# Hymba trunk layer on one core: another order of products, loads and final scaling in the down stage

## The chip, the core and the metric

The program runs on one NeuronCore of a Trainium2 chip. TensorE does the matrix products, VectorE and ScalarE the elementwise work, and SyncE (SP) issues the DMAs. The metric is the device time of one execution in microseconds (us), lower is better. Three runs of the kernel before took 2121.44 to 2122.35 us, with a median of 2121.78 us.

## The reference

One decoder layer on 512 tokens of width 2048, behind 16 meta tokens, in float32:

```python
h = concatenate([meta, x])
h = h + hybrid_mixer(rmsnorm(h, norm_mix), w_in, b_f, conv_w, out_gain, w_out)
h = h + (silu(f @ w_gate) * (f @ w_up)) @ w_down      # f = rmsnorm(h, norm_ffn), D_FF = 5632
out = rmsnorm(h, final_norm)[16:]                      # y * rsqrt(mean(y*y) + 1e-6) * final_norm
```

The change concerns the product with `w_down` (5632 x 2048) and the last rmsnorm.

## The kernel before

Weights come from DRAM in blocks of 1 MB through a ring of three buffers (`wpool`, pool 0). Each block is used in units of 128 x 1024 elements: ScalarE writes a rounded part `hi` (line 145), VectorE the rest `lo` (line 146), and every float32 product is made of three matmuls (lines 174 to 176). Both the gate and up stage and the down stage multiply 2 x 2 blocks by Strassen's method in Winograd's form, that is seven products of sums and differences of blocks instead of eight.

The gate and up stage ends with its result in seven linear combinations ("forms") per group of rows, which it writes to DRAM; the down stage reads form number `o` into a tile `x{o}` (`load_form`, line 744). Each of the five groups of 1024 rows of `w_down` is worked off in two halves `q` of the columns. A half has four weight blocks, "11", "12", "21" and "22", and seven products; each has two units of twelve matmuls with 512 columns. The first half of the first group runs in the order `FIRST_DOWN`: product 1 needs block "11" and tile `x0`, product 2 block "21" and `x5`, product 7 blocks "12" and "22" and `x1`, product 3 block "22" and `x6`. Which blocks a product's sum takes is in `NEEDS`, and `last` says after which product a block's buffer is free.

The blocks alternate, three by three, between pool 0 and a second ring of three buffers, `wpool3` (pool 2), which exists only once the gate and up stage has given back its memory (line 1025). `load_to` loads ahead as far as buffers are free. So of the first half three blocks are loaded while gate and up still runs, and the fourth, "22", later.

All DMAs stand in the one queue of SP, which works strictly in the order written into the program: an instruction that waits holds up those behind it. A scheduler places the instructions of all engines at build time; its order need not be that of the source, and the pieces of it that matter here are shown with the change.

The last 512 rows of `w_down` go through plain products (`down_last`), each piece of 128 rows by 512 columns followed by `finish`. There ScalarE squares and sums it (line 798). Once a 128-row group `t` has all its pieces, a few instructions on 128 x 1 elements make the factor `l_`. For the groups 0 to 2 VectorE then scales four pieces by `l_` and the norm weights in one instruction each (line 819). The last group multiplies by the norm weights piece by piece (line 807) and shares the scaling between VectorE and ScalarE (lines 821 and 823). SP issues all output DMAs (line 824).

Of the kernel before, what the change touches and what calls it, by code (L numbers as in the profile page):

```python
# [12 lines left out]
ALU = mybir.AluOpType  # L13
AX = mybir.AxisListType

P = 128
# [14 lines left out]
RAW_BUFS = 3  # L31
# [4 lines left out]
def hymba_kernel(  # L36
# [17 lines left out]
    nc = tc.nc  # L54
    x = x[0]
    w_in, w_out, w_gate, w_up, w_down = (w[0] for w in (w_in, w_out, w_gate, w_up, w_down))
    out = out[0]

    const = ctx.enter_context(tc.tile_pool(name="const", bufs=1))
    wpool = ctx.enter_context(tc.tile_pool(name="wpool", bufs=RAW_BUFS))  # L60
# [31 lines left out]
    def later(*stages):  # L92
        pending.extend((state["done"], s) for s in stages)

    pools = [wpool, None, None]
    held = [[], [], []]
    bufs = (RAW_BUFS, 1, RAW_BUFS)

    def add_block_of(view, k, f, pool=0):
        blocks.append({"src": view, "k": k, "f": f, "pool": pool})  # L100
        return len(blocks) - 1
# [545 lines left out]
    def ring():  # L647
        return 2 * ((len(blocks) - n_gate_up_blocks) // 3 % 2)
# [1 line left out]

    TARGETS = {1: (1, 0, 1), 2: (1, 0, 1), 6: (0, 0, 1), 4: (0, 0, 1), 7: (0, 1, -1), 5: (0, 1, -1), 3: (1, 1, -1)}

    FIRST_DOWN = ((1, 1, "a"), (2, 6, "b"), (7, 2, "c"), (6, 3, "a"), (4, 4, "c"), (5, 5, "a"), (3, 7, "d"))
    NEEDS = {1: ("11",), 2: ("21",), 7: ("12", "22"), 6: ("12", "22"), 4: ("12", "22", "21"), 5: ("12",), 3: ("22",)}

    def down(c):
        for q in range(2):
            bs = {}
            for b in ("11", "22", "12", "21") if c or q else ("11", "21", "12", "22"):
                h, f0 = int(b[0]) - 1, q * 1024 + (int(b[1]) - 1) * 512  # L660
                view = w_down[c * 1024 : (c + 1) * 1024, f0 : f0 + 512].rearrange("(p two k) f -> two k p f", two=2, k=P)[h]
                bs[b] = add_block_of(view, NPAIR, 512, ring())
            down_products(c, q, bs)

    def down_products(c, q, bs):
        cell, touched = {}, set()
        order = GATE_UP if c or q else FIRST_DOWN

        def source(i, half):
            def part(b):  # L670
                return blocks[bs[b]]["view"][:, 2 * half : 2 * half + 2, :]

            def add(o, a, b):
                nc.vector.tensor_tensor(o, a, b, op=ALU.add)
                return o

            if i == 7:
                cell["sum", half] = shared["dsums"].tile([P, 2, 512], F32, tag=f"sum{half}", name=f"sum{half}")
                return add(cell["sum", half], part("12"), part("22"))
            if i == 6:  # L680
                return add(cell["sum", half], cell["sum", half], part("11"))
            if i == 4:
                return add(cell["sum", half], cell["sum", half], part("21"))
            if i == 5:
                return add(part("12"), part("12"), part("11"))
            return part({1: "11", 2: "21", 3: "22"}[i])

        def product(n, i, o, b, half, hi, lo):
            if half == 0 and c == q == 0:
                load_soon(n)  # L690
            start = b not in cell
            if start:
                cell[b] = [bank("mm" if b in "ad" else "aux") for _ in range(2)]
            x = form_tiles[c, o]
            for k in range(2):
                kp = 2 * half + k
                for j in range(2):
                    ts = slice(j * P, (j + 1) * P)
                    mm3(cell[b][j], (x[:, 0, kp, ts], x[:, 1, kp, ts]), (hi[:, k, :], lo[:, k, :]), start and k == 0, i in (2, 3, 4) and kp == NPAIR - 1, skip_group_check=True)
            if half == 0:  # L700
                return
            for a, f, sign in [TARGETS[i]] + [TARGETS[3]] * (i == 5 and order is FIRST_DOWN):
                if (a, 2 * q + f) not in accs:
                    accs[a, 2 * q + f] = shared["down"].tile([P, 2, 512], F32, tag=f"acc{a}{2 * q + f}", name=f"acc{a}{2 * q + f}")
                for j in range(2):
                    m = acc(2 * a + j, 2 * q + f)
                    if c == 0 and (a, f) not in touched:
                        nc.scalar.activation(m, cell[b][j], AF.Copy, scale=float(sign))
                    else:
                        nc.vector.tensor_tensor(m, m, cell[b][j], op=ALU.add if sign > 0 else ALU.subtract)  # L710
                touched.add((a, f))
            if q == 1:
                load_form(c + 1, o)
                if c == NDOWN - 1 and n in (1, 3, 5):
                    add_h(*((0, 0), (1, 0), (0, 1))[n // 2])

        last = {"11": 5, "12": 5, "21": 2, "22": 3} if c or q else {"11": 5, "12": 5, "21": 4, "22": 3}
        for n, (i, slot, b) in enumerate(order):
            for half in range(2):
                add_unit(bs["11"], slice(0, 2), slice(0, 512), lambda hi, lo, a=(n, i, slot - 1, b, half): product(*a, hi, lo), sum=lambda i=i, half=half: source(i, half), also=[bs[m] for m in NEEDS[i]], look=4)  # L720
        for b, i in last.items():
            blocks[bs[b]]["last"] = len(units) - 14 + 2 * [g[0] for g in order].index(i) + 1

    def after_block(n):

        return tc.issue_after(blocks[min(n, state["loaded"] - 1)]["dma"].ins)

    def load_soon(n):

        if n == 0:  # L730
            with after_block(n_gate_up_blocks + 3):
                load_form(0, 2)
                load_form(0, 3)
        elif n == 2:
            with after_block(n_gate_up_blocks + 4):
                load_form(0, 4)
                load_form(0, 6)

    form_tiles = {}

# [4 lines left out]
    def load_form(c, o):  # L745
        if c < NDOWN:
            x = x_tile(o).rearrange("p (n k t) -> p n k t", n=2, k=NPAIR)
            nc.sync.dma_start(x.bitcast(F32), shared["forms"][c][o])
            form_tiles[c, o] = x
        elif o < 2:  # L750
            last_hid[o] = x_tile(o).rearrange("p (k t) -> p k t", k=4)
            nc.sync.dma_start(last_hid[o].bitcast(F32), shared["last"][o])
# [39 lines left out]
    def finish(t, fb, cols, n, last):  # L792

        tail, fss = shared["tail"], shared["fss"][:, t, :]
        a = acc(t, fb)[:, cols]
        fnorm = shared["fnorm"]
        r = shared["rstd2c"][:, t : t + 1]
        nc.scalar.activation(shared["sq"][:, cols], a, AF.Square, scale=r, accum_out=fss[:, n : n + 1])
        end = t == NT - 1
        if last:  # L800
            u, v, h, l_, lr = (tail.tile([P, 1], F32, tag=tag, name=tag) for tag in ("fu", "fv", "fh", "fl", "fr"))
            nc.vector.reduce_sum(u, fss[:, :n], axis=AX.X)
            nc.vector.tensor_scalar(u, u, 1.0 / D, EPS, op0=ALU.mult, op1=ALU.add)
            nc.scalar.activation(l_, fss[:, n : n + 1], AF.Ln, bias=u, scale=1.0 / D)
            nc.vector.scalar_tensor_tensor(v, fss[:, n : n + 1], 1.0 / D, u, op0=ALU.mult, op1=ALU.add)
        if end:
            nc.vector.tensor_tensor(a, a, fnorm[:, fb * 512 + cols.start : fb * 512 + cols.stop], op=ALU.mult)
        if not last:
            return
        nc.scalar.activation(l_, l_, AF.Exp, scale=-0.5)  # L810
        nc.scalar.activation(lr, l_, AF.Copy, scale=r)
        nc.vector.tensor_scalar(h, v, -0.5, None, op0=ALU.mult)
        nc.vector.scalar_tensor_tensor(h, h, l_, l_, op0=ALU.mult, op1=ALU.mult)
        nc.vector.scalar_tensor_tensor(l_, h, 1.5, lr, op0=ALU.add, op1=ALU.mult)
        parts = ((0, 0, 256), (0, 256, 512), (1, 0, 512), (2, 0, 512), (3, 0, 512)) if end else [(f, 0, 512) for f in range(4)]
        for n, (f, a, b) in enumerate(parts):
            o = acc(t, f)[:, a:b]
            if not end:
                nc.vector.scalar_tensor_tensor(o, o, l_, fnorm[:, f * 512 : (f + 1) * 512], op0=ALU.mult, op1=ALU.mult)
            elif n % 2:  # L820
                nc.scalar.activation(o, o, AF.Copy, scale=l_)
            else:
                nc.vector.tensor_scalar(o, o, l_, None, op0=ALU.mult)
            nc.sync.dma_start(out[t * P : (t + 1) * P, f * 512 + a : f * 512 + b], o)

    for pair in range(D_FF // 256):
        gate_up(pair)
# [192 lines left out]
    shared["down"] = ctx.enter_context(tc.tile_pool(name="down", bufs=1, reuse_waits="tile"))  # L1020
    load_form(0, 0)
    load_form(0, 5)
    with after_block(n_gate_up_blocks + 2):
        load_form(0, 1)
    pools[2] = ctx.enter_context(tc.tile_pool(name="wpool3", bufs=RAW_BUFS, side="right", reuse_waits="tile"))
    shared["dsums"] = ctx.enter_context(tc.tile_pool(name="dsums", bufs=1, side="right", reuse_waits="tile"))
    shared["tail"] = ctx.enter_context(tc.tile_pool(name="tail", bufs=2, side="right", reuse_waits="tile"))
# [36 lines left out]
```

## Time and profile before

| | |
|---|---|
| median of the runs | 2121.78 us |
| the profiled execution's own time | 2121.52 us |
| its span | 2119.7 us |
| TensorE busy | 2093.8 us (99%) |
| VectorE busy | 1588.9 us (75%) |
| ScalarE busy | 925.2 us (44%) |
| DMA, mean over the span | 146 GB/s |

Times within the trace are counted from the start of the span. The chain that ended last belongs to TensorE for 93% of the span, so time is gained or lost where TensorE waits, and after its last matmul. Most of the program is a stretch in which it never waits; the two places that the change touches are the start of the down stage, at 1679 us, and the end, from 2064 us on.

### The profile page before, as it was taken

How to read it: one execution, taken by the hardware profiler on the slowest of the kernel's cores; microseconds unless marked ns; L12 is line 12 of the kernel's file. 1: busy time of each engine (PE TensorE's matmuls, PEld its weight loads, DVE VectorE, ACT ScalarE, POOL GpSimd, SP SyncE). 2: the span in 40 equal slices, each digit the busy share in tenths (PEclk: the TensorE clock that was granted, in tenths of full speed). 3: DMA queues.
4: the chain of work that ended last, by engine and by line, in shares of the span. 5: the costliest groups of instructions: out<-in, count | busy, mean ns of one | idle time of the engine just before them, and what ended most of it. 6: DMA issues, size and time to landing. Idle time of an engine off the chain costs nothing.

```text
span 2119.7 us, 34563 instructions
## 1 busy us (share of the span) xinstructions
PE 2093.8 (99%) x14556; PEld 1937.0 (91%) x14556; DVE 1588.9 (75%) x2071; ACT 925.2 (44%) x1252; POOL 25.9 (1%) x78
## 2 busy tenths in 40 slices
PE   8999999999999999999999999999999999999997
PEld 7999999999998887999999999999999988888886
DVE  4756656454446667888898888888988798988996
ACT  5233334222215554544554455445544454333343
POOL 0000100000000000000000000000000000000000
PEclk9999999999999999999999999999999999999999
DMA  6322222232323433445444454454444665665562
GB/s 196 103 65 91 85 85 80 80 100 80 100 92 127 158 120 107 143 150 179 151 157 151 155 175 143 149 181 147 159 153 155 231 258 186 238 217 170 212 225 90
DMA packets 230751, 309.77 MB, mean 146 GB/s; under 512 B 7396, under 2 KB 183852, under 8 KB 225716
## 3 DMA queue, kind: packets, MB, share of 16 engines
q1 hardware_dynamic: 230596, 307.57, 43.7%
q8 instruction: 114, 1.87, 0.4%
q14 instruction: 41, 0.34, 0.1%
HBM read 260.35 MB, written 47.20 MB: 145 GB/s over the span
## 4 chain that ended last, share of the span: by engine, by line
PE 93%; DMA 2%; DVE 2%; ACT 1%; SPq 1%; issue 0%; DVEq 0%; ACTq 0%
PE mm L174 22%; PE mm L175 22%; PE mm L176 22%; PE mm L273 17%; PE aux L176 3%; PE aux L175 3%; PE aux L174 3%; DMA y<-in_x_dram 1%; DMA x<-forms_dram 1%; DVE lo L146 1%; DMA hin<-h_dram 1%; PE aux L374 1%; DVE acc L710 0%; PE aux L472 0%; ACT hf L481 0%
## 5 line engine op out<-in xcount | busy, mean ns | idle before, releaser
L145 ACT CAST hi<-raw 128x1024 fp32r<-128x1024 f32 x388 | 407.7, 1051 | 611.6 <-PE mm L175 266.7
L146 DVE TENSOR_TENSOR lo<-raw,hi 128x1024 fp32r<-128x1024 f32 x388 | 473.2, 1222 | 235.8 <-ACT hi L145 234.2
L176 PE MATMUL mm<-hhi,lo 128*128 128x256 f32 x1848 | 514.0, 278 | 0.6 <-DVE lo L146 0.6
L174 PE MATMUL mm<-hhi,hi 128*128 128x256 f32 x1848 | 505.8, 277 | 0.5 <-ACT gate L580 0.5
L175 PE MATMUL mm<-hlo,hi 128*128 128x256 f32 x1848 | 503.7, 276 | 0.0
L176 PEld LDWEIGHTS mm<-hhi,lo 128*128 128x128 f32 x1848 | 346.7, 188 | 2.5 <-DVE lo L146 0.8
L174 PEld LDWEIGHTS mm<-hhi,hi 128*128 128x128 f32 x1848 | 345.6, 188 | 2.0 <-ACT gate L580 2.0
L175 PEld LDWEIGHTS mm<-hlo,hi 128*128 128x128 f32 x1848 | 345.6, 188 | 0.0
L145 ACT CAST hi<-sum 128x1024 fp32r<-128x1024 f32 x192 | 201.6, 1051 | 307.0 <-DVE sum L533 159.7
L146 DVE TENSOR_TENSOR lo<-sum,hi 128x1024 fp32r<-128x1024 f32 x192 | 234.7, 1222 | 59.4 <-ACT hi L145 57.8
L273 PE MATMUL mm<-xhi,hi 128*128 128x256 f32 (+2 forms) x1024 | 215.4, 284 | 0.0
L273 PE MATMUL mm<-xhi,lo 128*128 128x256 f32 (+2 forms) x1024 | 214.0, 284 | 0.7 <-DVE lo L146 0.7
L273 PE MATMUL mm<-xlo,hi 128*128 128x256 f32 (+2 forms) x1024 | 214.0, 284 | 0.0
L174 PE MATMUL mm<-ghi,hi 128*128 128x256 f32 x616 | 172.7, 281 | 3.4 <-ACT ghi L145 3.3
L175 PE MATMUL mm<-glo,hi 128*128 128x256 f32 x616 | 171.8, 279 | 0.4 <-DVE glo L146 0.4
L176 PE MATMUL mm<-ghi,lo 128*128 128x256 f32 x616 | 170.8, 277 | 0.0
L273 PEld LDWEIGHTS mm<-xhi,hi 128*128 128x128 f32 x1024 | 163.3, 189 | 0.8
L273 PEld LDWEIGHTS mm<-xlo,hi 128*128 128x128 f32 x1024 | 162.1, 189 | 1.5 <-issue 0.9
L273 PEld LDWEIGHTS mm<-xhi,lo 128*128 128x128 f32 x1024 | 161.8, 189 | 1.4 <-DVE lo L146 0.9
L175 PE MATMUL mm<-lo,x 128*128 128x512 f32 x352 | 137.3, 390 | 0.6 <-DVE lo L146 0.6
L176 PE MATMUL mm<-hi,x 128*128 128x512 f32 x352 | 137.1, 389 | 0.0
L174 PE MATMUL mm<-hi,x 128*128 128x512 f32 x352 | 123.8, 389 | 1.1 <-DMA x<-forms_dram 1.1
(245 smaller groups left out, 3487.7 us busy)
## 6 DMA issues: line engine op xcount, KB each, us to landing
raw<-in_w_in_dram SPq DMA_DIRECT2D x47, 1024.0 KB, 5.3
raw<-in_w_gate_dram SPq DMA_DIRECT2D x44, 1024.0 KB, 4.8
raw<-in_w_up_dram SPq DMA_DIRECT2D x44, 1024.0 KB, 5.1
raw<-in_w_down_dram SPq DMA_DIRECT2D x44, 1024.0 KB, 6.4
x<-forms_dram SPq DMA_DIRECT2D x35, 1024.0 KB, 7.3
forms_dram<-fhi SPq DMA_DIRECT2D x20, 896.0 KB
forms_dram<-flo SPq DMA_DIRECT2D x20, 896.0 KB, 4.8
raw<-in_w_out_dram SPq DMA_DIRECT2D x16, 1024.0 KB, 5.0
```

Source lines behind the costliest of these rows:

```text
L145: nc.scalar.copy(hi, src)
L146: nc.vector.tensor_tensor(lo, src, f32(hi), op=ALU.subtract)
L174: nc.tensor.matmul(o, lhi, rhi, start=start, stop=False, **kw)
L175: nc.tensor.matmul(o, lhi, rlo, start=False, stop=False, **kw)
L176: nc.tensor.matmul(o, llo, rhi, start=False, stop=stop, **kw)
L273: nc.tensor.matmul(ps[:, : b - a], lhs[:, k, :], rhs[:, kt, a:b], start=s0, stop=s1)
L374: nc.tensor.transpose(ps[:, (i - i0) * P : (i - i0 + 1) * P], pr[i][:, j * P : (j + 1) * P], ident)
```

## The change

The first half of the first group now runs its products in the order 1, 2, 3, 7, 6, 4, 5. Its blocks are loaded in the order "11", "21", "22", "12", so that the three loaded ahead are those of the products 1, 2 and 3, and the fourth, "12", has a buffer of its own in the pool `down` (pool 3). The tiles loaded when that pool opens are `x0`, `x5` and `x6`, then block "12", and after these `x1` to `x4`. In `finish` every piece, not only those of the last group, is multiplied by the norm weights as it comes; the final scaling is shared by VectorE and ScalarE for all groups; and for the last group the two DMAs of ScalarE's pieces are issued by ScalarE.

```diff
--- before.py
+++ after.py
@@ -92,9 +92,9 @@
     def later(*stages):
         pending.extend((state["done"], s) for s in stages)
 
-    pools = [wpool, None, None]
-    held = [[], [], []]
-    bufs = (RAW_BUFS, 1, RAW_BUFS)
+    pools = [wpool, None, None, None]
+    held = [[], [], [], []]
+    bufs = (RAW_BUFS, 1, RAW_BUFS, 1)
 
     def add_block_of(view, k, f, pool=0):
         blocks.append({"src": view, "k": k, "f": f, "pool": pool})
@@ -650,16 +650,17 @@
 
     TARGETS = {1: (1, 0, 1), 2: (1, 0, 1), 6: (0, 0, 1), 4: (0, 0, 1), 7: (0, 1, -1), 5: (0, 1, -1), 3: (1, 1, -1)}
 
-    FIRST_DOWN = ((1, 1, "a"), (2, 6, "b"), (7, 2, "c"), (6, 3, "a"), (4, 4, "c"), (5, 5, "a"), (3, 7, "d"))
+
+    FIRST_DOWN = ((1, 1, "a"), (2, 6, "b"), (3, 7, "d"), (7, 2, "c"), (6, 3, "a"), (4, 4, "c"), (5, 5, "a"))
     NEEDS = {1: ("11",), 2: ("21",), 7: ("12", "22"), 6: ("12", "22"), 4: ("12", "22", "21"), 5: ("12",), 3: ("22",)}
 
     def down(c):
         for q in range(2):
             bs = {}
-            for b in ("11", "22", "12", "21") if c or q else ("11", "21", "12", "22"):
+            for b in ("11", "22", "12", "21") if c or q else ("11", "21", "22", "12"):
                 h, f0 = int(b[0]) - 1, q * 1024 + (int(b[1]) - 1) * 512
                 view = w_down[c * 1024 : (c + 1) * 1024, f0 : f0 + 512].rearrange("(p two k) f -> two k p f", two=2, k=P)[h]
-                bs[b] = add_block_of(view, NPAIR, 512, ring())
+                bs[b] = add_block_of(view, NPAIR, 512, ring() if c or q or b != "12" else 3)
             down_products(c, q, bs)
 
     def down_products(c, q, bs):
@@ -714,7 +715,7 @@
                 if c == NDOWN - 1 and n in (1, 3, 5):
                     add_h(*((0, 0), (1, 0), (0, 1))[n // 2])
 
-        last = {"11": 5, "12": 5, "21": 2, "22": 3} if c or q else {"11": 5, "12": 5, "21": 4, "22": 3}
+        last = {"11": 5, "12": 5, "21": 2, "22": 3} if c or q else {"11": 5, "12": 5, "21": 4, "22": 7}
         for n, (i, slot, b) in enumerate(order):
             for half in range(2):
                 add_unit(bs["11"], slice(0, 2), slice(0, 512), lambda hi, lo, a=(n, i, slot - 1, b, half): product(*a, hi, lo), sum=lambda i=i, half=half: source(i, half), also=[bs[m] for m in NEEDS[i]], look=4)
@@ -729,12 +730,12 @@
 
         if n == 0:
             with after_block(n_gate_up_blocks + 3):
+                load_form(0, 1)
                 load_form(0, 2)
-                load_form(0, 3)
         elif n == 2:
             with after_block(n_gate_up_blocks + 4):
+                load_form(0, 3)
                 load_form(0, 4)
-                load_form(0, 6)
 
     form_tiles = {}
 
@@ -803,8 +804,7 @@
             nc.vector.tensor_scalar(u, u, 1.0 / D, EPS, op0=ALU.mult, op1=ALU.add)
             nc.scalar.activation(l_, fss[:, n : n + 1], AF.Ln, bias=u, scale=1.0 / D)
             nc.vector.scalar_tensor_tensor(v, fss[:, n : n + 1], 1.0 / D, u, op0=ALU.mult, op1=ALU.add)
-        if end:
-            nc.vector.tensor_tensor(a, a, fnorm[:, fb * 512 + cols.start : fb * 512 + cols.stop], op=ALU.mult)
+        nc.vector.tensor_tensor(a, a, fnorm[:, fb * 512 + cols.start : fb * 512 + cols.stop], op=ALU.mult)
         if not last:
             return
         nc.scalar.activation(l_, l_, AF.Exp, scale=-0.5)
@@ -815,13 +815,12 @@
         parts = ((0, 0, 256), (0, 256, 512), (1, 0, 512), (2, 0, 512), (3, 0, 512)) if end else [(f, 0, 512) for f in range(4)]
         for n, (f, a, b) in enumerate(parts):
             o = acc(t, f)[:, a:b]
-            if not end:
-                nc.vector.scalar_tensor_tensor(o, o, l_, fnorm[:, f * 512 : (f + 1) * 512], op0=ALU.mult, op1=ALU.mult)
-            elif n % 2:
+            if n % 2:
                 nc.scalar.activation(o, o, AF.Copy, scale=l_)
             else:
                 nc.vector.tensor_scalar(o, o, l_, None, op0=ALU.mult)
-            nc.sync.dma_start(out[t * P : (t + 1) * P, f * 512 + a : f * 512 + b], o)
+            queue = nc.scalar if end and n % 2 else nc.sync
+            queue.dma_start(out[t * P : (t + 1) * P, f * 512 + a : f * 512 + b], o)
 
     for pair in range(D_FF // 256):
         gate_up(pair)
@@ -1020,8 +1019,11 @@
     shared["down"] = ctx.enter_context(tc.tile_pool(name="down", bufs=1, reuse_waits="tile"))
     load_form(0, 0)
     load_form(0, 5)
-    with after_block(n_gate_up_blocks + 2):
-        load_form(0, 1)
+    load_form(0, 6)
+
+    pools[3] = shared["down"]
+    assert state["loaded"] == n_gate_up_blocks + 3
+    load_part(1)
     pools[2] = ctx.enter_context(tc.tile_pool(name="wpool3", bufs=RAW_BUFS, side="right", reuse_waits="tile"))
     shared["dsums"] = ctx.enter_context(tc.tile_pool(name="dsums", bufs=1, side="right", reuse_waits="tile"))
     shared["tail"] = ctx.enter_context(tc.tile_pool(name="tail", bufs=2, side="right", reuse_waits="tile"))
```

In the built program the places that follow read thus. First the queue of SP where the down stage begins, before the change. `raw` is a weight block (`raw_17822` the third of the stage, `raw_17917` the fourth, "22"), `x0` to `x6` are the forms' tiles, `last_dram` takes the last rows of the gate and up result (`fhi` and `flo`).

```order
L123 DMA raw_17822<-in_w_down_dram 128x4x512
L748 DMA x0_17900<-forms0_dram_6690 128x2048
L748 DMA x5_17902<-forms0_dram_6690 128x2048
L748 DMA x1_17904<-forms0_dram_6690 128x2048
L123 DMA raw_17917<-in_w_down_dram 128x4x512
L123 DMA raw_17919<-in_w_down_dram 128x4x512
L623 DMA last_dram_6689<-fhi_17885 128x1024
L123 DMA raw_17921<-in_w_down_dram 128x4x512
L748 DMA x2_17927<-forms0_dram_6690 128x2048
L623 DMA last_dram_6689<-flo_17886 128x1024
L748 DMA x3_17929<-forms0_dram_6690 128x2048
L748 DMA x4_18009<-forms0_dram_6690 128x2048
```

And the same place after the change, where `raw_17906` is the block "12" in its own place, and `raw_17919`, `raw_17921` and `raw_18199` are blocks of `wpool3` for the second half and the group behind it.

```order
L123 DMA raw_17822<-in_w_down_dram 128x4x512
L123 DMA raw_17919<-in_w_down_dram 128x4x512
L123 DMA raw_17921<-in_w_down_dram 128x4x512
L123 DMA raw_18199<-in_w_down_dram 128x4x512
L623 DMA last_dram_6689<-fhi_17885 128x1024
L623 DMA last_dram_6689<-flo_17886 128x1024
L749 DMA x0_17900<-forms0_dram_6690 128x2048
L749 DMA x5_17902<-forms0_dram_6690 128x2048
L749 DMA x6_17904<-forms0_dram_6690 128x2048
L123 DMA raw_17906<-in_w_down_dram 128x4x512
L749 DMA x1_17927<-forms0_dram_6690 128x2048
L749 DMA x2_17929<-forms0_dram_6690 128x2048
```

`x0` and `x5` stood directly behind the third block, ahead of the first block of `wpool3`; now they stand behind three blocks of `wpool3` and both writes to `last_dram`, and block "12" and the other forms behind them.

Next VectorE at the end of the program, before: `acc_18474`, `acc_18239`, `acc_17961` and `acc_18158` hold the four column blocks of the last two row groups; `fu` to `fr` are 128 x 1.

```order
L814 SCALAR_TENSOR_TENSOR fl<-fh,fr 128x1
L807 TENSOR_TENSOR acc_18474<-acc_18474,fnorm 128x256
L802 TENSOR_REDUCE fu<-fss 128x1
L819 SCALAR_TENSOR_TENSOR acc_17961<-acc_17961,fl,fnorm 128x512
L819 SCALAR_TENSOR_TENSOR acc_18158<-acc_18158,fl,fnorm 128x512
L819 SCALAR_TENSOR_TENSOR acc_18239<-acc_18239,fl,fnorm 128x512
L819 SCALAR_TENSOR_TENSOR acc_18474<-acc_18474,fl,fnorm 128x512
L763 TENSOR_TENSOR acc_18474<-acc_18474,mm 128x256
L803 TENSOR_SCALAR fu<-fu 128x1
L805 SCALAR_TENSOR_TENSOR fv<-fss,fu 128x1
L807 TENSOR_TENSOR acc_18474<-acc_18474,fnorm 128x256
```

And after; `acc_18042` is what was `acc_18158`.

```order
L814 SCALAR_TENSOR_TENSOR fl<-fh,fr 128x1
L821 TENSOR_SCALAR acc_17961<-acc_17961,fl 128x512
L821 TENSOR_SCALAR acc_18239<-acc_18239,fl 128x512
L764 TENSOR_TENSOR acc_18474<-acc_18474,mm 128x256
L807 TENSOR_TENSOR acc_18239<-acc_18239,fnorm 128x512
L764 TENSOR_TENSOR acc_18474<-acc_18474,mm 128x256
L807 TENSOR_TENSOR acc_18474<-acc_18474,fnorm 128x256
L803 TENSOR_REDUCE fu<-fss 128x1
L807 TENSOR_TENSOR acc_18474<-acc_18474,fnorm 128x256
L804 TENSOR_SCALAR fu<-fu 128x1
L806 SCALAR_TENSOR_TENSOR fv<-fss,fu 128x1
L812 TENSOR_SCALAR fh<-fv 128x1
```

Four scalings by line 819 stood between the additions of the two last pieces; now two of line 821 stand ahead of both, and the multiplication of the last piece (the second `L807` of `acc_18474` with 256 columns) comes before the scalar `L804`.

Last, ScalarE at the end of the program after the change, with its two DMAs.

```order
L799 ACTIVATE sq,fss<-acc_18239,rfa 128x512
L819 ACTIVATE acc_18042<-acc_18042,fl 128x512
L819 ACTIVATE acc_18474<-acc_18474,fl 128x512
L799 ACTIVATE sq,fss<-acc_18474,rfa 128x256 x2
L805 ACTIVATE fl<-fss,fu 128x1
L810 ACTIVATE fl<-fl 128x1
L811 ACTIVATE fr<-fl,rfa 128x1
L819 ACTIVATE acc_17961<-acc_17961,fl 128x256
L819 ACTIVATE acc_18239<-acc_18239,fl 128x512
L823 DMA out_dram<-acc_17961 128x256
L823 DMA out_dram<-acc_18239 128x512
```

The two scalings of group 2 (`L819`) are ScalarE's now, and stand ahead of the squares of the two last pieces.

## Rows read from the trace of the kernel before

**Rows 1.** Busy time by engine in three stretches, first row the columns.

```profile
core 0: us, PE busy (x) PEld busy (x) DVE busy (x) ACT busy (x) POOL busy (x), PEclk, DMA share, GB/s
1679.00:1700.00 21.00, 18.28 (x78) 13.88 (x77) 16.09 (x17) 8.67 (x11) 0.00 (x0) 1.00 0.99 347
1700.00:2064.00 364.00, 364.00 (x1607) 301.34 (x1606) 326.45 (x344) 151.03 (x151) 0.00 (x0) 1.00 0.60 214
2064.00:2109.00 45.00, 43.83 (x204) 36.35 (x202) 30.21 (x60) 17.01 (x43) 0.00 (x0) 1.00 0.17 59
```

**Rows 2.** Timeline, TensorE, where the down stage starts: start, length, instruction, idle before.

```profile
...
1679.02 0.39 PE L174 MATMUL mm<-hi,x 128*128 128x512 f32 x1
...
1690.48 0.73 PE L174 MATMUL aux<-hi,x 128*128 128x512 f32 x2 [0.41 <-ACT hi L145]
...
1692.47 0.50 PE L175 MATMUL aux<-lo,x 128*128 128x512 f32 x1 [1.26 <-DVE lo L146]
...
1699.00 0.70 PE L174 MATMUL mm<-hi,x 128*128 128x512 f32 x2 [1.05 <-DMA x<-forms_dram]
...
```

**Rows 3.** Timeline, queue of SP, same place.

```profile
...
1668.71 3.15 SPq L748 DMA_DIRECT2D x<-forms_dram  x3
1679.21 0.93 SPq L123 DMA_DIRECT2D raw<-in_w_down_dram  x2
1680.75 0.34 SPq L623 DMA_DIRECT2D last_dram<-fhi  x1
1681.13 2.09 SPq L123 DMA_DIRECT2D raw<-in_w_down_dram  x1
1683.26 0.75 SPq L748 DMA_DIRECT2D x<-forms_dram  x1
...
```

**Rows 4.** Chain that ended last, 1678 to 1706: start, length, what.

```profile
...
1683.26 15.60 DMA x<-forms_dram
...
```

**Rows 5.** Line 123 (weight blocks), 1640 to 1760: from issue to landing.

```profile
...
DMA to landing us min/median/max: 5.9/6.2/14.3
```

**Rows 6.** Line 748 (forms), 1640 to 1760: from issue to landing.

```profile
...
DMA to landing us min/median/max: 4.8/6.4/8.1
```

**Rows 7.** Timeline, VectorE, where the down stage starts.

```profile
...
1681.38 0.68 DVE L146 TENSOR_TENSOR flo<-up,fhi 128x512 fp32r<-128x512 f32 x1
...
1687.79 2.36 DVE L674 TENSOR_TENSOR sum<-raw 128x1024 f32<-128x1024 f32 x2 [3.47 <-DMA raw<-in_w_down_dram]
...
```

**Rows 8.** Stretches before the gate and up stage, where TensorE had waited.

```profile
...
830.00:834.00 4.00, 1.29 (x4) 0.99 (x5) 3.00 (x5) 2.18 (x3) 0.00 (x0) 0.59 0.00 0
834.00:838.00 4.00, 3.59 (x9) 1.65 (x8) 3.97 (x8) 1.34 (x3) 0.00 (x0) 0.56 0.00 0
...
```

**Rows 9.** Timeline, TensorE, its last matmul.

```profile
...
2108.18 0.28 PE L176 MATMUL mm<-x,x 128*128 128x256 f32 x1
```

**Rows 10.** Timeline, VectorE, last rows.

```profile
...
2108.62 2.73 DVE L819 SCALAR_TENSOR_TENSOR acc<-acc,fl,fnorm 128x512 f32<-128x512 f32 x4
2111.27 0.41 DVE L763 TENSOR_TENSOR acc<-acc,mm 128x256 f32<-128x256 f32 x1
...
2112.43 0.42 DVE L807 TENSOR_TENSOR acc<-acc,fnorm 128x256 f32<-128x256 f32 x1
...
2113.54 1.15 DVE L823 TENSOR_SCALAR acc<-acc,fl 128x256 f32<-128x256 f32 x3
```

**Rows 11.** Timeline, ScalarE, last rows.

```profile
...
2106.35 0.72 ACT L798 ACTIVATE sq<-acc,rfa 128x512 f32<-128x512 f32 x1 [0.17 <-DVE acc L763]
...
2111.72 0.51 ACT L798 ACTIVATE sq<-acc,rfa 128x256 f32<-128x256 f32 x1 [3.54 <-DVE acc L763]
...
2112.35 0.30 ACT L804 ACTIVATE fl<-fss,fu 128x1 f32<-128x1 f32 x1
...
2113.54 1.12 ACT L821 ACTIVATE acc<-acc,fl 128x256 f32<-128x256 f32 x2 [0.33 <-DVE fl L814]
```

**Rows 12.** Timeline, queue of SP, last issues.

```profile
...
2113.92 2.54 SPq L824 DMA_DIRECT2D out_dram<-acc  x5
```

## The prediction

> **What bounds the kernel now.** I read the busy times by stretch first, then TensorE's gaps on the timeline, then the queue of SP beside them, and last the three engines at the end. In [rows 1] the reader is to see that from 1700 to 2064 us TensorE is busy for 364.00 of 364.00 us: what the change does to VectorE, ScalarE or DMA there costs nothing unless it makes TensorE wait. 1607 matmuls in 364 us are 0.2265 us each, so a product of 24 takes 5.44 us. In the 21 us from 1679 TensorE is busy for 18.28 only. [Rows 2] show the gaps: 0.41 and 1.26 us before the third product, 1.05 before the fourth, 2.72 us together. The first product, at 1679.02, has no gap before it. [Rows 7] tell why the third is late: VectorE's sum of "12" and "22" waits until 1687.79 for the fourth block, which SP issued at 1679.21 only [rows 3]. The gap before the fourth product is the DMA of a form issued at 1683.26, 15.60 us before it ended [rows 4]. The end lies behind the last matmul (2108.46 [rows 9]): VectorE first does four scalings of 2.73 us and adds the last piece at 2111.27 [rows 10].
>
> **The change where the down stage begins.** Products 1, 2 and 3 need only the three blocks that are loaded early, so the wait for the fourth block goes, and with it the wait for the next form: −2.72 us if nothing else comes late. But every product needs its form too, and there the order rows of SP decide. Before, `x0`, `x5` and `x1` were issued from 1668.71 on [rows 3], ten microseconds before TensorE read `x0`, and nothing held them. Then SP stood still until 1679.21, when the first block of `wpool3` went out. That is 0.03 us after the last matmul of gate and up, which started 0.11 us before the 1679.02 of [rows 2] and ran 0.28 us: the block takes memory that this matmul still read. After the change `x0` stands behind that block. Nothing on SP can pass it, so `x0` cannot be issued before 1679.2, when TensorE already wants it. Ahead of `x0` stand three blocks (3 MB), then the two writes to `last_dram` (0.5 MB each), the second of which waits for `flo`, ready at 1681.38 + 0.68 = 1682.1 [rows 7].
>
> When does `x0` land? The first block, with the queue empty before it, needs the median 6.2 us [rows 5]: 1679.21 + 6.2 = 1685.4. The pace behind it I take from before. There the block issued at 1679.21 had landed by 1687.79 [rows 7], and behind it came a block, half a megabyte of `fhi`, a block and the form issued at 1683.26, which landed at 1683.26 + 15.60 = 1698.86 [rows 3, 4]. That is 3.5 MB in 11.1 us, 3.16 us per MB. After the change 4 MB stand behind the first block up to and with `x0` (two blocks, two writes, the form): 12.7 us, so `x0` lands at 1685.4 + 12.7 = 1698.1. The first product then starts 19.1 us later than at 1679.02. Bounds: if transfers did not queue behind each other, `x0` would be issued at about 1682.1 and land after the shortest time of a form, 4.8 us [rows 6], at 1686.9, 7.9 us late. If each of the three blocks took 6.2 us and the 2 MB behind them 6.3 us, it would be 1704.1, 25.1 us late. I take 19.1, since the transfers before ran in the same queue with nearly the same content.
>
> The Trainium skill, DMA: Bandwidth & Descriptors (Queues, rings and completion order), says that each DMA engine takes its descriptors in ring order, but that completion is not first in, first out for an issuing engine. By the first half the sum stands; by the second a form could overtake blocks. The 15.60 us of [rows 4] against 4.8 us for a form on its own speak for the first.
>
> Behind `x0` all later forms move too. `x5` and `x6` follow at 3.16 us each and their products at 5.44 us each, so they are in time. Block "12" is three megabytes behind `x0`, 9.5 us. VectorE takes its two sums (2.36 us [rows 7]) before the `lo` of product 3's first half (as long as one of the sums, 1.2 us): 13.1 us after `x0`, when two products need 10.9 us and the clock's 1.8 us (below) come on top, 12.7 us. I cost this wait at nothing; its upper bound, with "12" two microseconds later, is 2 us. `x1` to `x4` have the same margin or more.
>
> While TensorE waits, its clock falls. In [rows 8] it had waited and then worked for 3.59 of 4 us at a granted share of 0.56, that is most of the time at 1.2 GHz instead of 2.4. A restart of the same kind loses 4 × (1 − 0.56) = 1.8 us. Bounds: nothing, and 3.4 us if both rows (0.59 and 0.56 over 8 us) fell behind the restart.
>
> **The change at the end.** For the groups 0 to 2 twelve multiplications (0.42 us for 256 columns [rows 10], so up to 0.84 each) replace twelve scalings of 2.73 / 4 = 0.68 us, six short scalings come on VectorE and six on ScalarE. Until 2109 VectorE is busy for 30.21 and ScalarE for 17.01 of 45 us [rows 1], beside TensorE's matmuls, so this is hidden. What counts begins with the square at 2106.35 [rows 11]. ScalarE's order is now: that square, two scalings of group 2, the squares of the two last pieces. A square of 256 columns holds it 2112.35 − 2111.72 = 0.63 us, one of 512 columns 0.21 more. Two scalings take 1.12 + 0.21 = 1.33 us. So 2106.35 + 0.84 + 1.33 + 2 × 0.63 = 2109.8; the last addition, free now to follow the matmul at 2108.46 and 0.41 us long, is in time. Before, that was 2112.35. But now the last multiplication (0.42) and a small instruction (at most the 0.30 of line 804) stand between the square and the logarithm: 2110.5. From there to the scaling are 2113.54 − 2112.35 = 1.19 us, so 2111.7 instead of 2113.54, 1.8 us earlier. Behind it SP issued five outputs one by one in 2.54 us, until 2116.46 [rows 12]. Now SP issues three, done by about 2111.7 + 1.15 + 0.4 = 2113.3, and ScalarE two behind its 1.12 us. How long an issue takes on ScalarE this trace does not show. With SP's mean of 0.51 us each the end is 2113.8, a gain of 2.6 us; with SP's longest, 2.09 us [rows 3], it is 2117.0, a loss of 0.5. The megabyte itself must still pass, which may leave only the 1.8. I take −2.5, nearest to SP's own issues at this place, with −3.2 (SP's three alone) and +0.5 as bounds.
>
> The Trainium skill, DMA: Bandwidth & Descriptors (Issuing engines are not separate DMA queues), says that issuing from several engines saves only the time to issue. By that rule the second queue adds at most two issues of 0.51 us to the 1.8, 2.8 us in all.
>
> **Sum.** From the profiled execution's 2121.5 us: +19.1 (first form) +1.8 (clock) −2.7 (old gaps) −2.5 (end) = +15.7, so 2137.2. The median of the runs lies 0.26 above that execution: 2137.5 us. With all bounds on one side it would be 2121.8 + 7.9 − 2.7 − 3.2 = 2123.8, or 2121.8 + 25.1 + 3.4 + 2 + 0.5 = 2152.8 with the gaps back in another place.
>
> **The rivals.**
> - *The form overtakes.* The blocks ahead of `x0` are only beside it, and it lands within 4.8 to 8.1 us of an issue at 1682.1 to 1684: 1686.9 to 1692. The cost is then 7.9 to 13 us, with the clock and the gains +4.5 to +9.6: 2126 to 2131. For it speaks that forms issued one after another landed in 8.1 us at most where they could go early [rows 6]. Against it speaks the 15.60 us of [rows 4].
> - *The form is no bound (faster than before).* If `x0` were in its tile when gate and up ends, as before, both gains would stay: 2121.8 − 2.7 − 2.5 = 2116.6 us. The mechanism is the one that the change describes, three products from blocks at hand. It decides up to the point where the first wait is as long as both gains, 1679.0 + 5.2 = 1684.2. Against it: the shortest landing, 4.8 us, behind an issue that comes after `flo` is ready at 1682.1.
> - *The wait moves on.* The queue is slower than 3.16 us per MB since all seven forms and one more block are now in it at once. `x0` comes at 1704, and block "12" holds the third product for another 2 us: 2144 to 2150 us. For it: the 347 GB/s of [rows 1] are now wanted for 12 MB from 1679 on where there were 8. Against it: the queue is served in order, and what is added stands behind `x0`.
>
> **How the numbers follow.** The first, 2137.5 us with an own range of 2131 to 2144, has 0.77; the overtaking form 0.11; no bound at the form 0.05; the wait that moves on 0.07. The range of 8 in 10 is 2128 to 2144.5: it takes in the upper half of the overtaking case and the edge of the last. A measurement of this kernel can tell 0.2% (4.2 us) from no change. Faster by more than that (under 2117.5) is most of the third case, 0.04. Within it, up to 2126.0, is the rest of that case and the edge of the overtaking one, 0.04. Slower is 0.92.
>
> **What would show it.** In the profile after, TensorE has one gap of 14 to 25 us before the first matmul with 512 columns of the down stage, put down to a form's DMA. SP issues three blocks from 1679.2 on and the first form behind them. The granted clock falls in that stretch. Products 3 and 7 have no gap of a microsecond or more. From the last matmul to the end of the span it is about 2.5 us less than the 11.2 (2119.7 − 2108.46) of before. It would be wrong if the first form were issued before the last matmul of gate and up, or if TensorE's gap were under 8 us.

## The result and the profile after

The changed kernel takes 2137.69 us (median of four runs, 2135.67 to 2138.88); four runs of the kernel before on the same chip had a median of 2122.07 us. The ratio is 1.0068, with a 95% interval of 1.0056 to 1.0081: slower by 15.6 us. The profiled execution took 2138.88 us, with a span of 2137.1 us where before had 2119.7.

First TensorE's idle times in the changed kernel: for each kind of wait the sum, the count and the longest, in us, over the down stage.

```profile
engine line waited for: us in total, times, longest us
PE mm L174 <- DMA x<-forms_dram: 18.8, 1, 18.8
PE mm L175 <- DVE lo L146: 0.7, 1, 0.7
```

The three gaps of [rows 2] are gone; products 3 and 7 have none. One gap has come in their place. TensorE's timeline there (start, length, instruction, idle before and what ended it):

```profile
1681.33 0.28 PE L176 MATMUL mm<-ghi,lo 128*128 128x256 f32 x1
1700.39 0.79 PE L174 MATMUL mm<-hi,x 128*128 128x512 f32 x1 [18.78 <-DMA x<-forms_dram]
1700.98 0.63 PE L175 MATMUL mm<-lo,x 128*128 128x512 f32 x1
...
1704.39 0.63 PE L174 MATMUL mm<-hi,x 128*128 128x512 f32 x1
1704.82 0.50 PE L175 MATMUL mm<-lo,x 128*128 128x512 f32 x1
...
1707.00 0.39 PE L175 MATMUL mm<-lo,x 128*128 128x512 f32 x1
```

The last matmul of gate and up ends at 1681.6, and 18.8 us later the first product starts: it has waited for the DMA of a form. Behind the gap the matmuls first take 0.63 us each instead of 0.39. The queue of SP in the same stretch (start of the first issue, time over all of them):

```profile
1670.71 12.39 SPq L123 DMA_DIRECT2D raw<-in_w_down_dram  x4
1683.20 1.07 SPq L623 DMA_DIRECT2D last_dram<-fhi  x1
1684.50 0.48 SPq L623 DMA_DIRECT2D last_dram<-flo  x1
1685.04 2.08 SPq L749 DMA_DIRECT2D x<-forms_dram  x3
1687.51 0.38 SPq L123 DMA_DIRECT2D raw<-in_w_down_dram  x1
1691.49 8.28 SPq L749 DMA_DIRECT2D x<-forms_dram  x4
```

In [rows 3] three forms went out at 1668.71. Here one weight block goes out at 1670.71, the group of four lasts until 1683.10, then come both writes, and the first form at 1685.04, 3.4 us after TensorE has run out of matmuls. It is in use 15.4 us later. Of the group of four the last three, the blocks of `wpool3`, are issued from 1681.63 on, 0.02 us after the last matmul of gate and up has ended. What holds `x0` last is the second write, as the chain that ended last shows (start, length, what):

```profile
1683.87 0.61 DVE flo L146
1684.50 0.48 SPq L623
1685.04 15.31 DMA x<-forms_dram
```

The write of `flo` goes out as soon as `flo` is ready, 2.9 us after the last matmul of gate and up, and `x0` right behind it. The busy times by stretch (columns as in [rows 1]) show the clock and the bus meanwhile:

```profile
1679.00:1700.00 21.00, 2.60 (x23) 2.40 (x22) 5.16 (x8) 3.03 (x4) 0.00 (x0) 0.63 0.81 286
1700.00:1704.00 4.00, 3.61 (x9) 2.84 (x10) 0.00 (x0) 0.00 (x0) 0.00 (x0) 0.50 1.01 418
1704.00:1720.00 16.00, 16.00 (x70) 13.21 (x69) 12.79 (x13) 7.29 (x9) 0.00 (x0) 0.97 0.93 373
1720.00:2080.00 360.00, 360.00 (x1589) 297.74 (x1588) 322.70 (x339) 150.45 (x150) 0.00 (x0) 1.00 0.57 204
```

TensorE is busy for 2.60 of 21 us, where [rows 1] had 18.28. It restarts at a granted clock of 0.50, which is the level of 1.2 GHz. From 1720 on nothing waits again, as before from 1700.

Last the end: TensorE, VectorE, ScalarE with its two DMAs, and SP, from the last matmul on.

```profile
2128.27 0.28 PE L176 MATMUL mm<-x,x 128*128 128x256 f32 x1
```

```profile
2128.59 0.42 DVE L764 TENSOR_TENSOR acc<-acc,mm 128x256 f32<-128x256 f32 x1 [0.26 <-PE mm L176]
...
2129.67 0.43 DVE L807 TENSOR_TENSOR acc<-acc,fnorm 128x256 f32<-128x256 f32 x1 [0.17 <-ACT sq L799]
2130.01 0.15 DVE L804 TENSOR_SCALAR fu<-fu 128x1 f32<-128x1 f32 x1
...
2131.34 1.15 DVE L821 TENSOR_SCALAR acc<-acc,fl 128x256 f32<-128x256 f32 x3
```

```profile
2130.26 0.29 ACT L805 ACTIVATE fl<-fss,fu 128x1 f32<-128x1 f32 x1 [0.62 <-DVE fu L804]
...
2131.34 1.12 ACT L819 ACTIVATE acc<-acc,fl 128x256 f32<-128x256 f32 x2 [0.23 <-DVE fl L814]
2131.88 0.95 ACTq L823 DMA_DIRECT2D out_dram<-acc  x2
```

```profile
2121.58 11.44 SPq L823 DMA_DIRECT2D out_dram<-acc  x11
```

The scaling starts at 2131.34, 2.8 us behind the last matmul's end (2128.55); in [rows 9, 10] it was 5.1 us. SP's last issue ends at 2133.02 and ScalarE's at 2132.83, so the span ends 4.1 us behind SP's last issue. From the last matmul to the end of the span it is 8.5 us where it was 11.2.

So the spans differ by: +2.4 us before the down stage (gate and up ends at 1681.6 instead of 1679.2, spoken of at the very end), +18.9 us from the end of gate and up to the first product's start (18.78, and 0.16 that the two overlapped before), −1.3 us over the down stage (428.16 us from the first product's start to the last matmul's end, where it was 429.44), −2.7 us behind it. The sum is 17.4, which is 2137.1 − 2119.7.

### The profile page after: what moved, and what is told of

Same layout as the page of the kernel before. It is cut to its first block, busy times and chain, and to the rows that moved or that the text cites. A ratio compares the mean times of both kernels' runs of the same rounds, so it can differ in the third digit from the quotient of the medians.

```text
span 2137.1 us, 34565 instructions
## 1 busy us (share of the span) xinstructions
PE 2098.3 (98%) x14556; PEld 1942.0 (91%) x14556; DVE 1590.6 (74%) x2077; ACT 931.0 (44%) x1258; POOL 26.0 (1%) x78
## 4 chain that ended last, share of the span: by engine, by line
PE 95%; DVE 2%; DMA 2%; ACT 1%; SPq 0%; issue 0%; DVEq 0%; ACTq 0%
PE mm L174 22%; PE mm L175 22%; PE mm L176 22%; PE mm L273 17%; PE aux L176 3%; PE aux L175 3%; PE aux L174 3%; DMA y<-in_x_dram 1%; DMA x<-forms_dram 1%; DVE lo L146 1%; PE aux L374 1%; DMA hin<-h_dram 0%; DVE acc L711 0%; DVE acc L645 0%; PE aux L472 0%
## 5 line engine op out<-in xcount | busy, mean ns | idle before, releaser
L174 PE MATMUL mm<-hi,x 128*128 128x512 f32 x352 | 124.6, 392 | 18.8 <-DMA x<-forms_dram 18.8
```

The lines of the kernel that those rows point to most:

```text
L174: nc.tensor.matmul(o, lhi, rhi, start=start, stop=False, **kw)
```

## The experiments

My theory: the order in SP's queue decides. `x0` is issued too late since it stands behind a block of `wpool3`, which must wait for memory, and lands later still by what stands between. The rivals were that a form overtakes what stands ahead, that the products' new order or the block in its own place costs something itself, and that the changed end isn't a gain.

### Forms ahead of the blocks of `wpool3`

The changed kernel, with these blocks issued behind `x0`, `x5`, `x6` and block "12". Only the two writes to `last_dram` still stand ahead of `x0`.

```diff
-        b["dma"] = nc.sync.dma_start(b["view"][:, ks, :], b["src"][:, ks, :])
+        with tc.issue_after(state["behind"]) if b["pool"] == 2 and "behind" in state else ExitStack():
+            b["dma"] = nc.sync.dma_start(b["view"][:, ks, :], b["src"][:, ks, :])
...
-    load_part(1)
+    with tc.issue_after(state["form"].ins):
+        load_part(1)
+    state["behind"] = blocks[n_gate_up_blocks + 3]["dma"].ins
```

> The changed kernel with one edit to the order on SP: the three blocks of the second weight ring are issued behind the forms x0, x5, x6 and block 12; only the two writes of the last gate and up rows (1 MB) still stand ahead of x0, so x0 can be issued at about 1682 us. Theory (the wait is x0 standing in SP's queue behind the blocks): TensorE's gap before the first down product shrinks from 18.8 to about 9 us, and the time is 2138 - 10 = about 2128 us. Rival (the gap comes from the new order of products or the new pool, or forms overtake blocks anyway): gap and time stay at 18 to 19 us and 2137 to 2139 us.

Measured: 2126.86 us (2125.65 to 2128.35), ratio to before 1.0025 [1.0015, 1.0035]. TensorE's first product and the queue of SP in this version:

```profile
1688.14 0.79 PE L175 MATMUL mm<-hi,x 128*128 128x512 f32 x1 [9.89 <-DMA x<-forms_dram]
```

```profile
1679.81 0.34 SPq L624 DMA_DIRECT2D last_dram<-fhi  x1
1681.15 0.34 SPq L624 DMA_DIRECT2D last_dram<-flo  x1
1681.59 1.73 SPq L750 DMA_DIRECT2D x<-forms_dram  x3
```

`x0` is still issued only after the write of `flo`, 3.3 us after the last matmul of gate and up where the changed kernel had 3.4: the blocks hardly move its issue. But with three blocks fewer ahead it is in use 6.5 us after its issue, not 15.4. The same DMA is 8.8 us slower behind 3 MB of blocks, so it does not get past them. The busy times of the changed kernel agree: from 1679 to 1700 us 286 GB/s moved 6.0 MB, and `x0` with all that stands ahead of it (five transfers' worth of 1024 KB) is 5.2 MB of these. Of the gap's 18.8 us, 8.9 belong to the blocks and 9.9 to the issue behind `flo` and the form's own landing.

### The last two writes on another queue

The version above, with the last two writes to `last_dram` issued by ScalarE, so that nothing stands ahead of `x0` that waits.

```diff
-                nc.sync.dma_start(shared["last"][n, ...
+                (nc.scalar if pair == D_FF // 256 - 1 else nc.sync).dma_start(shared["last"][n, ...
```

> As the run before, and the two writes of the last gate and up rows are issued by ScalarE's queue, so that x0, x5 and x6 stand directly behind the third block on SP and nothing holds them before the last gate and up matmul. Theory: no gap before the first down product; the old gaps (3.3 us with the restarts behind them) and 2.8 us at the end are gained: 2122 - 6 = about 2116 us, faster than both kernels. Rival (something else than the queue holds the first product, or the fourth block comes late now): a gap of over 5 us remains, 2122 us or more.

Measured: 2116.24 us (2115.0 to 2119.58), ratio 0.9977 [0.9968, 0.9986]: faster than before. SP's queue, and the longest gap that TensorE has left at this place:

```profile
1667.94 2.00 SPq L750 DMA_DIRECT2D x<-forms_dram  x3
1669.98 9.36 SPq L124 DMA_DIRECT2D raw<-in_w_down_dram  x3
```

```profile
1695.75 0.69 PE L175 MATMUL aux<-hi,x 128*128 128x512 f32 x2 [1.05 <-DMA x<-forms_dram]
```

The forms are issued at 1667.94 and the first gap is gone. The products' order, the fourth block's own place and the new end are all still there, so none of them is what made the kernel slower. By the medians it is 21.5 us faster than the changed kernel, by a different order of the same DMAs, two of them on another queue.

### The new end alone

The kernel before with the changed `finish`.

```diff
-        if end:
-            nc.vector.tensor_tensor(a, a, fnorm[:, fb * 512 + cols.start : fb * 512 + cols.stop], op=ALU.mult)
+        nc.vector.tensor_tensor(a, a, fnorm[:, fb * 512 + cols.start : fb * 512 + cols.stop], op=ALU.mult)
...
-            nc.sync.dma_start(out[t * P : (t + 1) * P, f * 512 + a : f * 512 + b], o)
+            queue = nc.scalar if end and n % 2 else nc.sync
+            queue.dma_start(out[t * P : (t + 1) * P, f * 512 + a : f * 512 + b], o)
```

> The kernel before with the changed finish alone: every piece multiplied by the norm weights as it comes, scaling on VectorE and ScalarE, two last DMAs on ScalarE. Theory: from the last matmul to the end of the span 8.5 us instead of 11.3, nothing else: 2122 - 2.8 = about 2119.2 us. Rival (the twelve more multiplications delay VectorE beside TensorE's last pieces): the stretch from 2064 us to the last matmul grows by 1 us or more and takes the gain back, 2121 to 2123 us.

Measured: 2118.83 us (2118.13 to 2121.56), ratio 0.9989 [0.998, 0.9998], that is 2.5 us by the medians, with an interval from 0.4 to 4.2. Its last matmul, and the last wait of TensorE ahead of it, here and in the kernel before:

```profile
2110.85 0.28 PE L176 MATMUL mm<-x,x 128*128 128x256 f32 x1
```

```profile
2067.62 0.50 PE L175 MATMUL mm<-lo,x 128*128 128x512 f32 x1 [0.66 <-DVE lo L146]
```

```profile
2064.95 0.50 PE L175 MATMUL mm<-lo,x 128*128 128x512 f32 x1 [0.63 <-DVE lo L146]
```

The last matmul ends at 2111.13 and the span at 2119.8, 8.7 us where before had 11.2. From the wait's end to the last matmul's end it is 43.5 us in both, so the twelve more multiplications delay nothing there and the rival falls. The end is a gain by itself, and its size is near that of the changed kernel (2.7). The profiled execution is the slowest of the eleven: the granted clock falls in it to 0.58 from 40 to 44 us and to 0.57 from 1695 to 1699 us, ahead of all that was edited, so only its end is compared.

### The kernel before with its forms late

The reverse of the first two: in the kernel before, `x0`, `x5` and `x1` are issued behind the first three blocks of `wpool3`. Nothing else is changed.

```diff
-    load_form(0, 0)
-    load_form(0, 5)
-    with after_block(n_gate_up_blocks + 2):
-        load_form(0, 1)
     pools[2] = ...
+    for _ in range(3):
+        load_part(1)
+    with after_block(n_gate_up_blocks + 5):
+        for o in (0, 5, 1):
+            load_form(0, o)
```

> The kernel before with one edit: the first three blocks of the second weight ring are issued ahead of the forms x0, x5 and x1. Order of products, pools and finish are those of before. Theory (the queue alone makes the wait): x0 lands about 15.7 us after the last gate and up matmul (three blocks and x0, no writes ahead), the clock costs 2 us, the old gaps go (-3.3): 2122 + 14.5 = about 2136.5 us. Rival (the wait belongs to the new product order or pool): no gap before the first product, 2119 to 2122 us.

Measured: 2134.91 us (2134.55 to 2136.11), ratio 1.0064 [1.005, 1.0078]. TensorE's first product and SP's queue:

```profile
1694.04 0.80 PE L174 MATMUL mm<-hi,x 128*128 128x512 f32 x1 [16.32 <-DMA x<-forms_dram]
```

```profile
1666.82 12.39 SPq L123 DMA_DIRECT2D raw<-in_w_down_dram  x4
1679.26 1.14 SPq L748 DMA_DIRECT2D x<-forms_dram  x1
```

This order alone makes the kernel before 13.6 us slower by the medians, with a gap at the same place. The gap is 2.5 us shorter than the changed kernel's; here no write stands ahead of `x0`. This row also separates issue and queue: `x0` goes out at 1679.26, a little later than TensorE wants it, and is in use 14.8 us later with three blocks ahead and no write.

### One form more, and the logarithm earlier

The version with the writes on ScalarE, with `x1` too ahead of the blocks of `wpool3`, and the scalar of line 804 ahead of the last multiplication.

```diff
-    state["behind"] = blocks[n_gate_up_blocks + 3]["dma"].ins
+    with tc.issue_after(blocks[n_gate_up_blocks + 3]["dma"].ins):
+        load_form(0, 1)
+    state["behind"] = state["form"].ins
...
+        with tc.issue_after(mean.ins) if last else ExitStack():
+            nc.vector.tensor_tensor(a, a, fnorm[...], op=ALU.mult)
```

> The version with all three first forms ahead (e2_forms_first, 2116.24 us), with one form more, x1, issued ahead of the blocks of wpool3, and the small VectorE instruction that the logarithm waits for moved ahead of the last multiplication by the norm weights. Theory (the order in SP's queue decides every wait here, and the end hangs on the logarithm): TensorE's gap of 1.05 us, put down to a form, goes, with some 0.3 us of lower clock behind it, and the logarithm comes 0.4 us earlier: 2116.2 - 1.3 - 0.4 = about 2114.5 us. Rival (the wait only moves to the next thing in the queue, a block of wpool3 or a later form, and the end is set by the transfers of the output): no change, 2115.8 to 2116.6 us, with a gap of about 1 us at another product.

Measured: 2114.03 us (2113.69 to 2114.21), ratio 0.9965 [0.9951, 0.9978]. All that TensorE still waits for in the down stage, and ScalarE at the logarithm:

```profile
engine line waited for: us in total, times, longest us
PE mm L176 <- DVE lo L147: 0.6, 1, 0.6
```

```profile
2105.35 0.29 ACT L805 ACTIVATE fl<-fss,fu 128x1 f32<-128x1 f32 x1
```

The wait did not move on: the gap before product 7 is gone and no other has come. The logarithm follows the square with 0.1 us between where the changed kernel had 0.62. From the last matmul's end (2104.12) to the end of the span it is now 8.2 us; so of 0.4 us expected there, 0.3 arrived. Two things were changed at once; the trace tells them apart, the times don't. This is the fastest version, 7.9 us below before by the medians.

### All outputs from SP

The version with the writes on ScalarE, without ScalarE's two DMAs at the end.

```diff
-            queue = nc.scalar if end and n % 2 else nc.sync
-            queue.dma_start(out[t * P : (t + 1) * P, f * 512 + a : f * 512 + b], o)
+            nc.sync.dma_start(out[t * P : (t + 1) * P, f * 512 + a : f * 512 + b], o)
```

> The version e2_forms_first (2116.24 us) with the last five output DMAs all issued by SP, as in the kernel before, instead of three by SP and two by ScalarE. Theory of the prediction (the second issuing engine saves two issues of 0.5 us): the last issue ends about 1.0 us later, so 2117.2 us. Rival (the megabyte that must still pass sets the end, and the issues lie beside it): within 0.3 us of 2116.2 us. The end of the span behind the last matmul, 8.5 us in the changed kernel, tells the same: 9.5 us by the theory, 8.5 to 8.8 by the rival.

Measured: 2117.79 us (2115.54 to 2119.87), ratio 0.9981 [0.9972, 0.9989]. That interval and the one of the version with both queues, 0.9968 to 0.9986, overlap, so the times don't settle it. Nor does the profiled execution's own time, since its gap before product 7 was 1.66 us instead of 1.05. The end of its span can be compared: 9.0 us behind the last matmul's end (2108.58 to 2117.6), where it was 8.5 with both queues. SP's last issue:

```profile
2101.61 12.45 SPq L823 DMA_DIRECT2D out_dram<-acc  x13
```

It ends at 2114.06, and the span 3.5 us later. With both queues:

```profile
2098.93 11.45 SPq L824 DMA_DIRECT2D out_dram<-acc  x11
```

There SP's last issue ends at 2110.38, and the span 4.0 us later. Each theory had half of it: with two issues fewer SP is done 4.5 us behind the last matmul's end instead of 5.5, 1.0 us earlier, and 0.5 us of that reaches the end in this one pair of executions. That the transfers take the rest is likely, but was not measured. The Trainium skill, DMA: Bandwidth & Descriptors (Issuing engines are not separate DMA queues), allowed at most the time of issuing. That bound holds here: 0.5 us of 1.0.

## Why the prediction was right

Predicted were 2137.5 us, measured 2137.69; the range held it, and the mechanism is the one forecast. That the two lie only 0.2 us apart is luck: in the stretches that the change touches the sum is 0.7 us too high, the profiled execution has 2.4 us ahead of them that no term foresaw, and the four runs lie 3.2 us apart. Term by term:

- **The first form, +19.1 us.** The gap is 18.78 us, 18.9 against the start of the first product before. The form was said to land at 1698.1; with the 2.4 us by which everything before lies later in this profile, 1700.39 is 1698.0. The order rows gave the place of `x0` behind blocks and writes that wait, [rows 3, 4] gave the pace, and the kernel before with its forms late shows that this order suffices. I had put the second write at 1682.1; it is issued at 1684.50, which is the same 2.4 us.
- **The clock, +1.8 us.** Ten matmuls, from 1700.39 to 1704.82, take 4.43 us, where 10 × 0.2265 = 2.27 would do: 2.2 us. The estimate from [rows 8] is 0.4 short. It could have missed by more: behind the gap of 9.9 us in the first experiment thirteen matmuls run at the low level (1688.14 to 1693.85, 2.8 us lost), behind that of 16.3 us in the kernel before with its forms late only six (1694.04 to 1696.76, 1.4 us lost). The loss does not follow the length of the gap.
- **The old gaps, −2.7 us.** All three are gone. The down stage is 1.3 us shorter although the clock costs it 2.2, so 3.4 us have gone with them (1.28 + 2.16), 0.7 more than was put down. A gap's idle time is thus less than its cost. In [rows 2] one can see it: the matmul behind a gap takes 0.50 us where in the stream it takes 0.39, and two of them 0.70 and 0.73 where 0.39 + 0.23 would do. Besides, in the stream one starts every 0.23 us although it takes 0.39, so each gap also loses the overlap of 0.16 us, which the idle time leaves out.
- **The end, −2.5 us.** Measured −2.7 in the changed kernel and −2.5 with the changed `finish` alone. Its two parts: the scaling comes 2.3 us earlier behind the last matmul, where I had 1.8, and the second queue is worth about 0.5, where I had 0.7. About half of the first difference lies in the bound: I took ScalarE's own queue of scalings and squares, until 1.3 us behind the last matmul. In the trace the last square starts when the last addition ends (2128.59 + 0.42 = 2129.01), and ScalarE has read its sum 1.1 us behind that matmul:

```profile
2129.04 0.51 ACT L799 ACTIVATE sq<-acc,rfa 128x256 f32<-128x256 f32 x1
```

  SP's issues end 4.5 us behind the last matmul instead of 8.0 [rows 9, 12], 3.5 us earlier; but the span ends 4.1 us behind them instead of 3.2, so 0.8 are lost again behind the last issue.
- **Costs put at nothing.** Products 3 and 7 have no gap, so block "12" and `x1` were in time; the 2 us kept for them were not needed. By the prediction's own sum block "12" was 0.4 us late (13.1 against 12.7) and was still put at nothing. In the trace VectorE starts the sums that need it at 1707.87, 7.5 us behind the first product's start, so the block came at least 2 us sooner than the 9.5 reckoned.

The four errors are −0.2, +0.4, −0.7 and −0.2 us, −0.7 together, which is less than the runs scatter.

The rivals: *the form overtakes* falls by the first experiment, where the same DMA is 8.8 us quicker without the blocks ahead. By the Trainium skill, DMA: Bandwidth & Descriptors (Queues, rings and completion order), completion need not be in order; in no run here did a form get past the blocks. *The form is no bound* (2116.6 us) was the right price for a kernel in which `x0` is early: with the forms first it is 2116.24. *The wait moves on* has no gap to show for it.

## What to carry to other kernels

In this kernel an operand in the one queue that SP works off in order was as late as the latest instruction ahead of it: a block that waits for memory, or a write whose data come late. So after a reordering, list for each operand of the first product what now stands ahead of it in the built program, and which of these must wait for memory. Here a gain of 5 us was real in each of its parts and was hidden under a wait of 19, which was no part of the idea, and which an order of the same DMAs takes away. The pace of a queue is best read from the same queue in the trace of before, since the landing time of a transfer with little ahead of it (6.5 us here behind two writes) says little about the same one behind 3 MB more (15.4 us).

## What the runs showed of the hardware that was not expected

- The two DMAs issued by ScalarE took it 0.95 us, 0.48 each, as long as SP's at that place (0.51 by [rows 12]). This was the unknown of the end.
- Of the 2.4 us before the down stage, 1.5 are there by 100 us: an instruction of ScalarE (line 360, 528 columns) that starts at 99.65 us in the kernel before starts at 101.17. By 1000 us it is 2.0 us. In the profiled execution of the changed kernel the granted clock falls near the program's start; in the first experiment, whose code is the same at that place, it does not. The stretches 24 to 28 and 28 to 32 us of the changed kernel, then of the first experiment:

```profile
24.00:28.00 4.00, 2.49 (x13) 2.52 (x14) 1.98 (x2) 1.69 (x3) 0.00 (x0) 0.71 1.00 327
28.00:32.00 4.00, 4.00 (x30) 3.91 (x29) 2.25 (x3) 2.76 (x6) 0.00 (x0) 0.86 0.51 194
```

```profile
24.00:28.00 4.00, 3.86 (x32) 3.81 (x33) 3.69 (x5) 2.43 (x4) 0.00 (x0) 1.00 1.01 358
28.00:32.00 4.00, 4.00 (x25) 3.47 (x24) 0.26 (x1) 2.50 (x5) 0.00 (x0) 1.00 0.13 52
```

  TensorE is busy for 2.49 of the first 4 us there, and for 3.86 in the other. Why one execution waits longer at this place was not tried, and where the last 0.9 us come from stays open. The change is not needed for it: in the profile of the new end alone, whose code up to the last rows is that of before, the clock falls from 40 to 44 us and the same instruction starts at 101.94, 2.3 us late.
